# Matmul operands of an encoder layer placed at different remainders modulo 256 bytes

## The chip, the cores and the metric

The kernel runs on one core of a Trainium2 chip. The metric is the device time of one execution in microseconds (us), from the first to the last instruction with what lies around them. A core has five engines that run side by side: TensorE (PE, with weight loads shown as PEld), VectorE (DVE), ScalarE (ACT), GpSimd (POOL) and SyncE (SP), and 16 DMA engines. All of them meet in the on-chip memory SBUF: 128 partitions, and along each partition a row of bytes. This case is about where along that row a buffer starts.

## The reference

One layer of a bidirectional encoder, on 512 tokens of width 2048, in float32:

```python
xn = rmsnorm(h, norm1_g)
z_f, q, k, v, gate_f, gate_a = split(xn @ w_in)          # widths 1024, 2048 (five times)
y_f = Re(2-D DFT of z_f over tokens and channels of a group) @ w_fourier
y_a = rmsnorm(differential attention of q, k, v) * (1 - lambda_init) @ w_attn
h = h + (sigmoid(gate_f) * y_f + sigmoid(gate_a) * y_a) @ w_out
hn = rmsnorm(h, norm2_g)
# PEER: 8 heads, product keys, the best 16 of 16384 experts for each head and token
act = gelu(hn . expert_u[idx]) * softmax(top_scores)
h = h + sum(act * expert_v[idx])
```

## The kernel before

**Three matmuls for one.** Each float32 operand is split into a high part (rounded to the type fp32r, by a cast on ACT) and a low part (the rest, by a subtraction on DVE). `mm3` (lines 138 to 141) then issues three matmuls: high by high (L139), high by low (L140), low by high (L141). In a matmul the first operand is stationary: a weight load puts its 128 columns into the array. The second operand moves: its columns stream through the array. Rows of the trace write `out<-moving,stationary`, so `vb<-atl,whi` streams `atl` over weights `whi`. The weights of the next matmul are loaded while the present one streams.

**The stream of weights.** All weights come as 1 MB pieces (128 x 2048 float32) through one ring, made by `fetch`, `high`, `low` and `take`: `raw` (by DMA), `whi` (L112, ACT) and `wlo` (L117, DVE), three buffers each, in the pool `gran`. `take` hands out piece i, and has the high part of piece i+2 made, the low part of i+1, and piece i+4 fetched.

**The stages, in order.** Fourier branch, attention heads, gates, projections and queries: matmuls that write `mm`, with 512, 256 or 258 moving columns; the activations lie in `ah0..3` and `al0..3` (pool `act`), stationary in some stages and moving in others. Then the scores: 128 blocks of experts, of 48 matmuls each, `mm<-ah,whi` with 352 moving columns: the experts are evaluated densely for 352 of the 512 tokens. The other 160 gather their experts' rows by indirect DMA and work on them on DVE, beside these matmuls. The result of each block goes through gelu to the scratch `s_d`. Last the values: for each pair n of blocks `weigh` multiplies the scores `st` by the routing weights `gt` and casts the product to `ath` (L1027); `weigh_low` makes `atl` (L1033). Five buffers each, of two blocks (index `ee`) side by side:

```python
        h = pool.tile([P, 2, SD], F32R, name="ath", bufs=5)     # SD = 352 columns
        nc.scalar.copy(h, st)
```

They move through weights from `expert_v`, into eight PSUM banks `vb`; `add_up` (L1083) adds the banks to `accT`. In this stage too, DVE sums gathered rows (`acc`, L1073).

**Where the buffers start.** Pools stack tile after tile, and SBUF is full to its end. In the pool `act`, on the right end, a filler `shim` of 56 float32 lies behind the activations. Worked out from the tiles' sizes, these starts modulo 256 bytes follow (the first column of a slice within a `whi`, `wlo`, `ah` or `al` lies a multiple of 512 bytes behind the start of its tile):

| tile | before | after the change |
|---|---|---|
| whi (3 buffers) | 0, 0, 0 | 0, 64, 128 |
| wlo (3 buffers) | 0, 0, 0 | 64, 128, 128 |
| ah, al (4 each) | 0 | 128 |
| ath, ee = 0 (5 buffers) | 0 each | 0, 0, 0, 64, 224 |
| ath, ee = 1 | 128 each | 64, 64, 64, 128, 32 |
| atl, ee = 0 | 0 each | 0, 64, 128, 0, 160 |
| atl, ee = 1 | 128 each | 64, 128, 192, 64, 224 |
| raw (3 buffers), accT, acc, row | 0, 224, 224, 224 | the same |

Before, the half `ee` = 1 starts 352 columns or 1408 bytes, that is 5.5 times 256, behind the half `ee` = 0.

The order of the instructions is written out by hand, engine by engine (`manual_schedule`), so that waits alone move them in time.

Of the kernel before, what the change touches and what calls it, by code (L numbers as in the profile page):

```python
# [9 lines left out]
F32 = mybir.dt.float32  # L10
F32R = mybir.dt.float32r
# [5 lines left out]
P = 128  # L17
S = 512
D = 2048
# [12 lines left out]
SD = S - G0  # L32
# [3 lines left out]
COL = {2: 0, 3: P, 1: 2 * P, 0: 3 * P}  # L36
FH = 258
R = 8


@with_exitstack
def tile_encoder_layer(ctx: ExitStack, tc: tile.TileContext, x, g1, g2, qkg, sg, lv, nd, cs, cc,
                       w8, wz, wqkv, wgf, wga, wf, wa, wo, wq, keys, up, eu, ev, g2r, out):
    nc = tc.nc
# [6 lines left out]
    gran = pool_of(ctx, "gran", 3)  # L51
    act = pool_of(act_ctx, "act", side="right")
# [15 lines left out]
    def f32(ap):  # L68
        return ap.bitcast(F32)
# [20 lines left out]
                    "(e p) d -> p e d", p=P))  # L90
    raws, his, los, at, V = {}, {}, {}, [0], {}

    def fetch(i):
        if i < len(stream):
            raw = gran.tile([P, D], F32, name="raw")
            src = stream[i]
            nc.sync.dma_start(raw if len(src.shape) == 2 else raw.rearrange("p (a b) -> p a b", a=2), src)
            raws[i] = raw
# [8 lines left out]
    def high(i):  # L107
        if i in folds:
            fold(i)
        if i < len(stream):  # L110
            his[i] = gran.tile([P, D], F32R, name="whi")
            nc.scalar.copy(his[i], raws[i])  # L112

    def low(i):
        if i < len(stream):
            los[i] = gran.tile([P, D], F32R, name="wlo")
            nc.vector.tensor_sub(los[i], raws.pop(i), f32(his[i]))  # L117

    def take(k):
# [99 lines left out]
    dots2 = const.tile([P, G2], F32, name="dots2")  # L219
    qks = few[:, 11:11 + HEADS + 1]  # L220
    xnT = new_act()
    shim = act.tile([P, 56], F32, name="shim")
    nc.vector.memset(shim, 0.0)

    def first_group(pool, spare, junk, done):

        rows, guesses, rstd, banks = [], {}, {}, [bank("mm") for _ in range(4)]
        for tb in range(NT):
            rows.append(pool.tile([P, D], F32, name=f"x{tb}"))
            for i in range(2):  # L230
                sl = slice(i * 1024, i * 1024 + 1024)
                nc.sync.dma_start(rows[tb][:, sl], x[tb * P:(tb + 1) * P, sl])
            if tb == 0:
                fetch(0)
        nc.gpsimd.dma_start(g1s, g1)
        nc.gpsimd.dma_start(g2s, g2)
        nc.gpsimd.dma_start(sgs, sg)
        nc.gpsimd.dma_start(qkgs, qkg)
        fetch(1)
        fetch(2)  # L240

        def measure(tb):
            sums = pool.tile([P, 4], F32, name=f"xs{tb}")
            for i in range(4):
                square_sum(rows[tb][:, i * 512:(i + 1) * 512], sums[:, i:i + 1], junk)
            guesses[tb] = row_guess(pool, sums, f"n1{tb}")

        def rows_of(n):
            k4, tb = divmod(n, NT)
            return k4, tb, rows[tb][:, k4 * 512:k4 * 512 + 512]  # L250

        def scale(n):
            k4, tb, src = rows_of(n)
            if k4 == 0:
                rstd[tb] = rms_refine(guesses[tb])
            nc.vector.tensor_scalar(src, src, rstd[tb], None, op0=ALU.mult)

        def turn(n):
            src = rows_of(n)[2]
            turned[n] = bank("tr")  # L260
            for k in range(4):
                nc.tensor.transpose(turned[n][:, k * P:(k + 1) * P], src[:, k * P:(k + 1) * P], ident)

        def place(n):
            k4, tb, _ = rows_of(n)
            xg = spare[:, n % 2].rearrange("p (k t) -> p k t", k=4)
            nc.vector.tensor_tensor(xg, turned.pop(n).rearrange("p (k t) -> p k t", k=4),
                                    g1s[:, 4 * k4:4 * k4 + 4, None].to_broadcast([P, 4, P]), op=ALU.mult)
            h, l = xnT[k4]
            bs = slice(tb * P, (tb + 1) * P)  # L270
            split(xg, h[:, :, bs], l[:, :, bs])

        def quarter(i, q, parts="hl"):
            sl = slice(q * 512, q * 512 + 512)
            if i not in his:
                his[i], los[i] = gran.tile([P, D], F32R, name="whi"), gran.tile([P, D], F32R, name="wlo")
            if "h" in parts:
                nc.scalar.copy(his[i][:, sl], raws[i][:, sl])
            if "l" in parts:
                nc.vector.tensor_sub(los[i][:, sl], raws[i][:, sl], f32(his[i][:, sl]))  # L280
            if "l" in parts and q == 3:
                raws.pop(i)
                fetch(i + 3)

        turned = {}
        measure(0)
        for q in range(4):
            quarter(0, q, "h")
        scale(0)
        turn(0)  # L290
        quarter(0, 0, "l")
        place(0)
        for q in range(1, 4):
            quarter(0, q, "l")
        measure(1)
        plan = {(0, 3): "s1 t1 m2 p1", (1, 0): "s2 t2 m3 p2", (2, 0): "s3 t3 p3 s4 s5", (2, 2): "t4 p4",
                (3, 0): "t5 p5 s6 s7"}
        plan[12, 2] = "t15 p15"
        for n in range(4, 13):
            plan[n, 0] = f"t{n + 2} p{n + 2}" + (f" s{n + 4}" if n < 12 else "")  # L300
        for n in range(16):
            gi, tb = divmod(n, NT)
            if tb == 0 and gi < 3:
                wh, wl = (t.pop(gi).rearrange("p (k c) -> p k c", k=4) for t in (his, los))
                at[0] += 1
            elif tb == 0:
                wh, wl = take(4)
            bs = slice(tb * P, (tb + 1) * P)
            for kk in range(4):
                ah, al = kslice(xnT, gi * 4 + kk)  # L310
                mm3(banks[tb], (ah[:, bs], al[:, bs]), (wh[:, kk, :], wl[:, kk, :]),
                    gi == 0 and kk == 0, gi == 3 and kk == 3)
                for word in plan.get((n, kk), "").split():
                    i = int(word[1:])
                    {"s": scale, "t": turn, "p": place, "m": measure}[word[0]](i)
            if n in (2, 3):
                quarter(1, 2 * n - 4)
                quarter(1, 2 * n - 3)
            if 4 <= n < 12:
                quarter(n // 4 + 1, n % 4)  # L320
            if n == 11:
                high(4)
            if gi == 3:
                done(tb, banks[tb])
# [6 lines left out]
    with ExitStack() as so:  # L331
        with ExitStack() as st:
            pool = pool_of(st, "p1z")
# [687 lines left out]
    def weigh(n):  # L1021
        ck, e2 = pairs[n]
        st = sts[n]
        sv = st.rearrange("p e (c t) -> p e c t", t=GT)
        nc.vector.tensor_mul(sv, sv, gts[ck][:, :, 2 * e2:2 * e2 + 2, :].rearrange("p c e t -> p e c t"))
        h = pool.tile([P, 2, SD], F32R, name="ath", bufs=5)
        nc.scalar.copy(h, st)  # L1027
        ats[n] = h

    def weigh_low(n):  # L1030
        h, st = ats[n], sts.pop(n)
        l = pool.tile([P, 2, SD], F32R, name="atl", bufs=5)
        nc.vector.tensor_sub(l, st, f32(h))  # L1033
        ats[n] = (h, l)

    load_weights(0)
# [55 lines left out]
    for i in range(NE):  # L1092
        ck, j = divmod(i, R)
        half, e2 = divmod(j, R // 2)
        vh, vl = take(2)
        for job in owed:
            add_up(*job)
        owed = []
        if e2 == 0:
            banks = []  # L1100
        h, l = ats[ck * 4 + e2]
        for dt in range(8):
            ds_ = slice(dt * P, dt * P + P)
            if e2 == 0:
                banks.append(vps.tile([P, 512], F32, name="vb")[:, :SD])
            for ee in range(2):
                mm3(banks[dt], (vh[:, ee, ds_], vl[:, ee, ds_]), (h[:, ee, :], l[:, ee, :]),
                    e2 == 0 and ee == 0, e2 == R // 2 - 1 and ee == 1)
        n = ck * 4 + made[j] if j in made else len(pairs)
        if n < len(pairs):  # L1110
            weigh(n)
        if j == 2 and ck > 0:
            load_weights(ck + 1)
        given += shares[j]
        gather.to(given / total)
        if n < len(pairs):
            weigh_low(n)
            load_scores(n + 3)
        if e2 == R // 2 - 1:
            for dt in range(4):  # L1120
                add_up(ck, half, dt, banks[dt])
            owed = [(ck, half, dt, banks[dt]) for dt in range(4, 8)]
        if i == NE - 4:
            gather.to(1.0)
            for t0, n, col in ((2 * P - G2, G2, None), (2 * P, P, COL[2]), (3 * P, P, COL[3]), (P, P - G2, COL[1])):
                row = accp.tile([P, D], F32, name="row", bufs=4)
                nc.sync.dma_start(row[:n], rows_d[t0:t0 + n])
                finals.append((t0, n, col, row))
# [113 lines left out]
```

## Time and profile before

| | us |
|---|---|
| median of 3 runs (3842.77, 3864.57, 3866.42) | 3864.57 |
| the profiled execution: its own time | 3845.72 |
| its span, from the first to the last instruction | 3843.9 |
| PE busy in the span | 3792.6 |
| DVE busy | 2621.2 |
| ACT busy | 1457.9 |

The three runs lie in two places, some 22 us apart; the profiled execution agrees with the lower. A matmul's row shows a duration of some 320 ns, but matmuls are pipelined: the next one starts 155 to 165 ns behind. The pace of PE is therefore read from the starts, or from how many matmuls fall into a window, and not from the durations. A count in a window takes in about two more than the window's length holds, those that reach over its edges.

### The profile page before, as it was taken

How to read it: one execution, taken by the hardware profiler on the slowest of the kernel's cores; microseconds unless marked ns; L12 is line 12 of the kernel's file. 1: busy time of each engine (PE TensorE's matmuls, PEld its weight loads, DVE VectorE, ACT ScalarE, POOL GpSimd, SP SyncE). 2: the span in 40 equal slices, each digit the busy share in tenths (PEclk: the TensorE clock that was granted, in tenths of full speed). 3: DMA queues.
4: the chain of work that ended last, by engine and by line, in shares of the span. 5: the costliest groups of instructions: out<-in, count | busy, mean ns of one | idle time of the engine just before them, and what ended most of it. 6: DMA issues, size and time to landing. Idle time of an engine off the chain costs nothing.

```text
span 3843.9 us, 53562 instructions
## 1 busy us (share of the span) xinstructions
PE 3792.6 (99%) x22055; PEld 3528.4 (92%) x22055; DVE 2621.2 (68%) x3759; ACT 1457.9 (38%) x1966; POOL 684.5 (18%) x415
## 2 busy tenths in 40 slices
PE   8999999999999999999999999999999999999999
PEld 6888888888888888889999999999999999999998
DVE  5544465555523342578996887897758999999995
ACT  4322333333322122323237638837933223223231
POOL 0000011111100000000241232232213323332330
PEclk9999999999999999999999999999999999999999
DMA  4333222222234342425998898998989999999994
GB/s 165 111 142 135 71 83 99 73 82 83 83 105 152 121 153 99 164 91 172 360 372 299 317 365 315 346 364 314 329 311 389 360 368 371 356 378 368 376 358 166
DMA packets 214188, 900.11 MB, mean 234 GB/s; under 512 B 16556, under 2 KB 94476, under 8 KB 132108
## 3 DMA queue, kind: packets, MB, share of 16 engines
q1 hardware_dynamic: 145856, 519.34, 36.8%
q0 software_dynamic: 46960, 339.81, 22.7%
q10 hardware_dynamic: 21128, 37.53, 2.7%
q8 instruction: 174, 2.85, 0.3%
q14 instruction: 70, 0.57, 0.0%
HBM read 831.31 MB, written 65.27 MB: 233 GB/s over the span
## 4 chain that ended last, share of the span: by engine, by line
PE 91%; issue 3%; DMA 2%; ACT 2%; DVE 1%; POOL 0%; ACTq 0%; DVEq 0%; SPq 0%; POOLq 0%
PE mm L139 20%; PE mm L141 20%; PE mm L140 20%; PE vb L139 8%; PE vb L140 8%; PE vb L141 8%; PE tr L872 2%; DMA g_d<-gs 1%; PE tr L139 1%; PE tr L140 1%; PE tr L141 1%; ACT whi L112 0%; DMA row<-in_ev_dram,idx 0%; PE tr L564 0%; ACT rb L888 0%
## 5 line engine op out<-in xcount | busy, mean ns | idle before, releaser
L112 ACT CAST whi<-raw 128x2048 fp32r<-128x2048 f32 x395 | 754.3, 1910 | 1277.6 <-PE vb L140 387.0
L117 DVE TENSOR_TENSOR wlo<-raw,whi 128x2048 fp32r<-128x2048 f32 x395 | 901.8, 2285 | 320.4 <-ACT whi L112 319.7
L139 PE MATMUL mm<-ah,whi 128*128 128x352 f32 (+1 forms) x3072 | 1080.1, 352 | 0.0
L141 PE MATMUL mm<-ah,wlo 128*128 128x352 f32 (+1 forms) x3072 | 1061.9, 346 | 6.5 <-DVE wlo L117 6.5
L140 PE MATMUL mm<-al,whi 128*128 128x352 f32 (+1 forms) x3072 | 1061.9, 346 | 0.0
L139 PE MATMUL vb<-ath,whi 128*128 128x352 f32 x2048 | 660.6, 323 | 1.6 <-ACT accT L1081 1.6
L141 PE MATMUL vb<-ath,wlo 128*128 128x352 f32 x2048 | 655.6, 320 | 1.2 <-DVE wlo L117 1.2
L140 PE MATMUL vb<-atl,whi 128*128 128x352 f32 x2048 | 655.9, 320 | 0.0
L141 PEld LDWEIGHTS mm<-ah,wlo 128*128 128x128 f32 x3072 | 579.4, 189 | 47.2 <-DVE wlo L117 6.8
L140 PEld LDWEIGHTS mm<-al,whi 128*128 128x128 f32 x3072 | 580.9, 189 | 39.1
L139 PEld LDWEIGHTS mm<-ah,whi 128*128 128x128 f32 x3072 | 580.2, 189 | 39.0 <-issue 0.2
L139 PE MATMUL mm<-whi,ah 128*128 128x512 f32 (+1 forms) x1408 | 502.1, 357 | 3.1 <-ACT ah L129 3.1
L141 PE MATMUL mm<-whi,al 128*128 128x512 f32 (+1 forms) x1408 | 495.9, 352 | 0.0
L140 PE MATMUL mm<-wlo,ah 128*128 128x512 f32 (+1 forms) x1408 | 495.1, 352 | 0.0
L139 PEld LDWEIGHTS vb<-ath,whi 128*128 128x128 f32 x2048 | 384.0, 188 | 1.9 <-ACT accT L1081 1.9
L141 PEld LDWEIGHTS vb<-ath,wlo 128*128 128x128 f32 x2048 | 383.7, 187 | 1.7 <-DVE wlo L117 1.7
L140 PEld LDWEIGHTS vb<-atl,whi 128*128 128x128 f32 x2048 | 384.7, 188 | 0.0
L1066 POOL DMA_INDIRECT row<-in_ev_dram,idx x128 | 246.1, 1923 | 468.6 <-DVE acc L1073 445.4
L1073 DVE SCALAR_TENSOR_TENSOR acc<-row,w,acc 128x2048 f32<-128x2048 f32 x128 | 300.5, 2347 | 12.3 <-DMA row<-in_ev_dram,idx 11.1
L141 PEld LDWEIGHTS mm<-whi,al 128*128 128x128 f32 x1408 | 267.0, 190 | 37.4 <-DVE al L130 0.7
L139 PEld LDWEIGHTS mm<-whi,ah 128*128 128x128 f32 x1408 | 267.2, 190 | 36.3 <-ACT ah L129 3.8
L140 PEld LDWEIGHTS mm<-wlo,ah 128*128 128x128 f32 x1408 | 267.7, 190 | 33.0
(323 smaller groups left out, 3708.3 us busy)
## 6 DMA issues: line engine op xcount, KB each, us to landing
raw<-in_up_dram SPq DMA_DIRECT2D x128, 1024.0 KB
raw<-in_ev_dram SPq DMA_DIRECT2D x128, 1024.0 KB
raw<-in_wqkv_dram SPq DMA_DIRECT2D x48, 1024.0 KB
s_d<-ge ACTq DMA_DIRECT2D x128, 176.0 KB
g_d<-gs SPq DMA_DIRECT2D x22, 1024.0 KB
gt<-g_d SPq DMA_DIRECT2D x16, 1408.0 KB
st<-s_d SPq DMA_DIRECT2D x64, 352.0 KB
raw<-in_wgf_dram SPq DMA_DIRECT2D x16, 1024.0 KB
```

Of the source, the lines that this page charges most:

```text
L112: nc.scalar.copy(his[i], raws[i])
L117: nc.vector.tensor_sub(los[i], raws.pop(i), f32(his[i]))
L139: nc.tensor.matmul(ps, ah, bh, start=first, stop=False, skip_group_check=shared)
L140: nc.tensor.matmul(ps, ah, bl, start=False, stop=False, skip_group_check=shared)
L141: nc.tensor.matmul(ps, al, bh, start=False, stop=last, skip_group_check=shared)
L872: nc.tensor.matmul(ps[:, t % 4], rb, ra, start=True, stop=True)
L1066: nc.gpsimd.indirect_dma_start(out=rows[s], out_offset=None, in_=ev, in_offset=bass.IndirectOffsetOnAxis(ap=jobs[s][0], axis=0))
L1073: nc.vector.scalar_tensor_tensor(acc, rows.pop(s), w, acc, op0=ALU.mult, op1=ALU.add)
```

## The change

Every buffer of `whi`, `wlo`, `ath` and `atl` becomes a tile with a name of its own and one buffer, used in the same turn as before (i modulo 3, n modulo 5). Between some of them lie fillers (`gap`, each written once by a memset on DVE), by `HGAP`, `LGAP` and two fillers of 64 bytes in `gran`. `shim` gives up the 128 bytes that these two take, and all between the two ends, `ah` and `al` too, moves by 128. The two halves of `ath` and `atl` are 400 instead of 352 columns apart, and each is made by an instruction of its own.

```diff
+HGAP = [4, 2, 0, 0, 1]
+LGAP = [2, 4, 6, 0, 0]
...
+    def gap(pool, name, n):
+        if n:
+            nc.vector.memset(pool.tile([P, 8 * n], F32, name=name, bufs=1), 0.0)
+
+    def part(name, i):
+
+        if (name, i) in (("wlo", 0), ("wlo", 1)):
+            gap(gran, f"gap{i}", 2)
+        return gran.tile([P, D], F32R, name=f"{name}{i % 3}", bufs=1)
...
-            his[i] = gran.tile([P, D], F32R, name="whi")
+            his[i] = part("whi", i)
...
-            los[i] = gran.tile([P, D], F32R, name="wlo")
+            los[i] = part("wlo", i)
...
-    shim = act.tile([P, 56], F32, name="shim")
+    shim = act.tile([P, 24], F32, name="shim")
...
-        h = pool.tile([P, 2, SD], F32R, name="ath", bufs=5)
-        nc.scalar.copy(h, st)
+        k = n % 5
+        if n < 5:
+            gap(pool, f"hgap{k}", HGAP[k])
+        h = pool.tile([P, 2 * SD + 48], F32R, name=f"ath{k}", bufs=1)
+        h = [h[:, :SD], h[:, SD + 48:]]
+        for ee in range(2):
+            nc.scalar.copy(h[ee], st[:, ee])
         ats[n] = h
...
-        l = pool.tile([P, 2, SD], F32R, name="atl", bufs=5)
-        nc.vector.tensor_sub(l, st, f32(h))
+        k = n % 5
+        if n < 5:
+            gap(pool, f"lgap{k}", LGAP[k])
+        l = pool.tile([P, 2 * SD + 48], F32R, name=f"atl{k}", bufs=1)
+        l = [l[:, :SD], l[:, SD + 48:]]
+        for ee in range(2):
+            nc.vector.tensor_sub(l[ee], st[:, ee], f32(h[ee]))
...
-                mm3(banks[dt], (vh[:, ee, ds_], vl[:, ee, ds_]), (h[:, ee, :], l[:, ee, :]),
+                mm3(banks[dt], (vh[:, ee, ds_], vl[:, ee, ds_]), (h[ee], l[ee]),
```

On DVE, towards the end of the stage of the values, this stands in a row before (`acc` is the sum of gathered rows, `iw` holds their weights):

```order
L1083 TENSOR_TENSOR accT<-vb,accT 128x352 x4
L1025 TENSOR_TENSOR st<-st,gt 128x704
L1073 SCALAR_TENSOR_TENSOR acc_23815<-row,iw_91,acc_23815 128x2048
L1033 TENSOR_TENSOR atl<-st,ath 128x704
L117 TENSOR_TENSOR wlo<-raw,whi 128x2048
```

and at the same place now:

```order
L1106 TENSOR_TENSOR accT<-vb,accT 128x352 x4
L1038 TENSOR_TENSOR st<-st,gt 128x704
L1096 SCALAR_TENSOR_TENSOR acc_23831<-row,iw_91,acc_23831 128x2048
L1056 TENSOR_TENSOR atl_31384<-st,ath_31378 128x352 x2
L130 TENSOR_TENSOR wlo_31391<-raw,whi_31311 128x2048
```

Nothing has moved; the subtraction of 704 columns has become two of 352, in the same place ahead of the next `wlo`. On ACT, in the same stage, before:

```order
L1027 CAST ath<-st 128x704
L112 CAST whi<-raw 128x2048 x4
L1027 CAST ath<-st 128x704
L112 CAST whi<-raw 128x2048
L1027 CAST ath<-st 128x704
```

and now:

```order
L1045 CAST ath_30909<-st 128x352 x2
L125 CAST whi_30923<-raw 128x2048
L125 CAST whi_30985<-raw 128x2048
L125 CAST whi_31046<-raw 128x2048
L125 CAST whi_31115<-raw 128x2048
L1045 CAST ath_31170<-st 128x352 x2
L125 CAST whi_31181<-raw 128x2048
```

Here too only the cast to `ath` is in two. The matmuls stand on PE in the same order as before, and POOL and SP issue the same.

## Rows read from the trace of the kernel before

**Rows 1.** The page: busy us and instructions; DMA in 40 slices.

```profile
PE 3792.6 (99%) x22055; PEld 3528.4 (92%) x22055; DVE 2621.2 (68%) x3759; ACT 1457.9 (38%) x1966; POOL 684.5 (18%) x415
...
DMA  4333222222234342425998898998989999999994
```

**Rows 2.** Groups of instructions on PE, shapes apart: xcount, busy us, mean ns, idle before.

```profile
L139 PE MATMUL mm<-ah,whi 128*128 128x352 f32 x2048 | 678.6, 331 | 0.0
...
L139 PE MATMUL vb<-ath,whi 128*128 128x352 f32 x2048 | 660.6, 323 | 1.6 <-ACT accT L1081 1.6
...
L141 PE MATMUL vb<-ath,wlo 128*128 128x352 f32 x2048 | 655.6, 320 | 1.2 <-DVE wlo L117 1.2
L139 PE MATMUL mm<-ah,whi 128*128 128x512 f32 x1024 | 401.5, 392 | 0.0
...
L139 PE MATMUL mm<-whi,ah 128*128 128x512 f32 x896 | 356.7, 398 | 3.1 <-ACT ah L129 3.1
...
L139 PE MATMUL mm<-whi,ah 128*128 128x256 f32 x512 | 145.4, 284 | 0.0
```

**Rows 3.** Windows: busy us and count by engine, clock, DMA share.

```profile
412.00:428.00 16.00, 16.00 (x136) 16.00 (x135) 7.72 (x11) 2.74 (x3) 2.98 (x1) 1.00 0.38 132
1140.00:1500.00 360.00, 360.00 (x1590) 298.06 (x1590) 119.20 (x82) 88.75 (x67) 0.00 (x0) 1.00 0.36 132
1755.00:1815.00 60.00, 60.00 (x374) 60.00 (x373) 53.65 (x133) 20.89 (x20) 3.48 (x3) 1.00 0.53 178
2185.00:2270.00 85.00, 85.00 (x534) 85.00 (x533) 82.55 (x105) 29.58 (x26) 29.84 (x16) 1.00 0.97 371
3000.00:3400.00 400.00, 400.00 (x2519) 400.00 (x2518) 364.51 (x280) 117.14 (x78) 133.31 (x68) 1.00 0.94 370
```

**Rows 4.** Timeline of PE where the granted clock was 0.5: start, us.

```profile
1829.03 0.49 PE L141 MATMUL mm<-ah,wlo 128*128 128x352 f32 x1
1829.32 0.49 PE L139 MATMUL mm<-ah,whi 128*128 128x352 f32 x1
1829.62 0.49 PE L140 MATMUL mm<-al,whi 128*128 128x352 f32 x1
```

**Rows 5.** Timeline of PE in the stage of the values: half ee = 1, then ee = 0.

```profile
3400.32 0.32 PE L139 MATMUL vb<-ath,whi 128*128 128x352 f32 x1
3400.48 0.32 PE L140 MATMUL vb<-atl,whi 128*128 128x352 f32 x1
3400.63 0.32 PE L141 MATMUL vb<-ath,wlo 128*128 128x352 f32 x1
3400.79 0.32 PE L139 MATMUL vb<-ath,whi 128*128 128x352 f32 x1
3400.95 0.32 PE L140 MATMUL vb<-atl,whi 128*128 128x352 f32 x1
3401.12 0.32 PE L141 MATMUL vb<-ath,wlo 128*128 128x352 f32 x1
3401.27 0.32 PE L139 MATMUL vb<-ath,whi 128*128 128x352 f32 x1
```

**Rows 6.** Timeline of PE in an attention head: twelve matmuls, first and last start.

```profile
458.58 0.28 PE L140 MATMUL tr<-vl,aTh 128*128 128x256 f32 x1
...
459.89 0.39 PE L139 MATMUL mm<-whi,ah 128*128 128x512 f32 x1
```

**Rows 7.** Timeline of PE in the Fourier stage: ten matmuls, first and last.

```profile
186.94 0.28 PE L140 MATMUL mm<-yl,whi 128*128 128x258 f32 x1
...
188.03 0.28 PE L140 MATMUL mm<-yl,whi 128*128 128x258 f32 x1
```

**Rows 8.** Groups on DVE in the stage of the values.

```profile
L1083 DVE TENSOR_TENSOR accT<-vb,accT 128x352 f32<-128x352 f32 x239 | 115.3, 519 | 61.1 <-PE vb L141 59.0 <-issue 1.5
...
L1033 DVE TENSOR_TENSOR atl<-st,ath 128x704 fp32r<-128x704 f32 x62 | 55.1, 889 | 38.3 <-ACT ath L1027 38.2
```

**Rows 9.** Groups on ACT in the same stage.

```profile
L1027 ACT CAST ath<-st 128x704 fp32r<-128x704 f32 x62 | 48.1, 776 | 7.6 <-DVE st L1025 7.6
L1081 ACT COPY accT<-vb 128x352 f32<-128x352 f32 x16 | 6.2, 460 | 0.9 <-PE vb L141 0.9
```

**Rows 10.** The window of that stage.

```profile
2848.00:3827.00 979.00, 976.21 (x6141) 975.34 (x6140) 856.84 (x648) 289.41 (x205) 307.04 (x161) 1.00 0.91 354
```

More of the change, by code (lines that the diff above doesn't have):

```diff
@@ L275, in quarter @@
             if i not in his:
-                his[i], los[i] = gran.tile([P, D], F32R, name="whi"), gran.tile([P, D], F32R, name="wlo")
+                his[i], los[i] = part("whi", i), part("wlo", i)
             if "h" in parts:
```

## The prediction

> **What bounds the kernel now.** Read the page first: PE is busy for 99% of the span [rows 1]. Then the groups on PE: nearly no idle time stands before them [rows 2]. So PE's own pace is the time, and this change, which leaves the matmuls and their order as they are, can only act through the spacing of one matmul from the next. That spacing is read from windows in which PE never idles: length by count, less the two at the edges. Five of them [rows 3]: 16.0/134 = 119.4 ns with 256 moving columns, 360/1588 = 226.7 with 512, 60/372 = 161.3 and 85/532 = 159.8 with 352 (early and later in the scores), and 400/2517 = 158.9 with 352 in the values. The granted clock there is 1.00, the level of 2.4 GHz, at which a column each cycle would be 106.7, 213.3 and 146.7 ns. What is above that I call the excess: 12.7, 13.4, 14.6, 13.1 and 12.2 ns. At the other level there is none: with the clock at 0.5 the starts are 0.29 to 0.30 us apart [rows 4], and 352 columns at 1.2 GHz are 293.3 ns. So some 13 ns of each matmul are lost at the full clock alone, and not to columns. Of all spacings there are 6144 of the scores, 6144 of the values, 3072 + 2688 with 512 columns and 1536 with 256 (three lines for each group of rows 2): 19,584 matmuls, some 250 us of excess.
>
> **Does the excess depend on placement?** Before the change nearly all operands start at remainder 0. The one large exception is the half ee = 1 in the values, at 128. There the spacings aren't alike: 0.16, 0.15, 0.16, 0.16, 0.17, 0.15, with 0.95 us for six [rows 5], where the scores, same shape and all at 0, take 0.96 or 0.97 by their windows [rows 3]. Three matmuls of six have a moving start that differs from that of their weights, and the mean is 160.0 - 158.9 = 1.1 ns lower. Two smaller places point both ways. In the heads the moving `vh`, `vl` start at 192 and the stationary parts at 64 (from their tiles' sizes): (459.89 - 458.58)/11 = 119.1 ns, an excess of 12.4 [rows 6]. In the Fourier stage the moving parts start at steps of 8 bytes from 64 to 152 against weights at 0: (188.03 - 186.94)/9 = 121.1 ns for 258 columns, an excess of 13.6 [rows 7]. And the two windows of the scores differ by 1.5 ns with the very same addresses [rows 3]: a rhythm between loads and streams can, it seems, lock in two ways. So placement matters, by one or two ns, and no row shows a place where it matters by much more for long.
>
> The Trainium skill says otherwise: its page "TensorE: Matmul & The Clock Gate", Part 2, Step-by-step, gives PE two independent read ports in SBUF, so that loading the next weights takes nothing from the running matmul. By that rule starts would not matter at all, and the sum below would be 0. The trace doesn't agree: the spacings of rows 5 vary with the half.
>
> **The change part by part.**
>
> *The matmuls.* I price a matmul whose moving and stationary starts differ, against one whose starts agree, by the values before: 1.1 ns on average with half of them unequal, so 2.2 ns each. Counting the pairs after the change from the starts: in the scores moving 128 meets weights at 0, 64, 128, and 3440 of 6144 pairs (56%) are unequal; with 512 columns 1568 of 3072 and 1312 of 2688; with 256 columns 1280 of 1536; in the values 4696 of 6144 (76%), before it was 3072. Gains: scores 3440 x 2.2 = 7.6 us; 512 columns 2880 x 2.2 = 6.3; 256 columns 1280 x 2.2 = 2.8; values (4696 - 3072) x 2.2 = 3.6. The early scores ran in the slower rhythm [rows 3], I take it a quarter of them; with six weight buffers at three starts I expect that lock to break: 1536 x 1.3 = 2.0 us. Sum 22.3 us. Bounds: were every spacing of 352 columns the shortest that recurs [rows 5] (0.15 us as rounded; I take 155 ns), it would be 5 ns x 13,440 for all that are at remainder 0 now and 3.9 x 6144 in the values, 91 us less; were all in the slow rhythm, 161.3, it would be 1.3 x 13,440 + 2.4 x 6144 = 32 us more. I stay near the values' average and not near either end, as it alone is a mean over thousands of matmuls with mixed starts.
>
> *Two instructions for one.* A subtraction of 704 columns takes 889 ns on DVE, one of 352 at most the 519 of the addition to accT, which has an operand in PSUM [rows 8]: 2 x 519 - 889 = 149 ns more, 62 times in this stage, 9.2 us. On ACT 2 x 460 - 776 = 144 ns [rows 9], 62 times, 8.9 us. From below both are 0, since columns stay the same and a second start costs something. I take the upper ends. DVE has 979 - 857 = 122 us idle in the stage, ACT 690 [rows 10]; behind `atl` on DVE queue the next `wlo`, for which PE waited only 1.2 us [rows 2], made more than a block (48 x 159 = 7.6 us) ahead. So nothing of it lies on PE's path; were that cover gone, DVE's 9.2 us would be the price.
>
> *Fillers.* Eight memsets of at most 48 columns, each below the 519 ns of 352 columns [rows 8]: under 4 us on DVE, once, hidden likewise. The names with one buffer each are reused after the same number of turns as before, so no wait is added; POOL and SP have the same queues. DMA is busy for 0.94 to 0.97 of the two late windows [rows 3], so a PE faster by more than about 4% would meet it; 22 us are 0.6%.
>
> **Sum.** The profiled execution took 3845.7 us; less 22 it is 3824. The median of the three runs is 3864.6, 19 above the profiled one; on that footing 3842, which I give as the forecast.
>
> **The rivals.**
>
> *Conflicts nearly gone.* If agreement of starts between the load and the stream is the whole cause of the excess and the new starts keep them apart, the spacing goes to 155 or below everywhere: 91 us, 3774 on the median's footing; half of that, 3819, already counts here. For it: one recurring step of the values is there, and the excess is absent at the lower clock, so there is something to remove. Against it: 44% of the pairs in the scores still agree, and in rows 7 no start agrees and the excess is 13.6.
>
> *Placement is free* (or: one excess goes where another came). Rows 6 and 7 speak for it, with 12.4 and 13.6 on either side of the 13.3 at equal starts. Then the time is the median, 3865, give or take what separates the runs. The Trainium skill's rule above ("TensorE: Matmul & The Clock Gate", Part 2) would give this.
>
> *A slower rhythm everywhere.* The early scores kept the rhythm of 161.3 through a window of 60 us with starts as in the later one [rows 3]. If mixed starts put most of the scores and values into such a rhythm, or into the 13.6 of rows 7 and above, PE loses 32 us (3897 on the median's footing). It decides from a mean excess above 13.3 ns in the scores. Against it: the values, where starts mix, are the fastest of the 352-column windows.
>
> **How the numbers follow.** A measurement of this kernel can tell about 1%, 39 us, from no change. The forecast (-10 to -38 us) gets 0.35; conflicts nearly gone (beyond -38) 0.33; placement free (-10 to +10) 0.2; slower rhythm 0.12, most of it below 39 us as well, the rest by a rhythm still slower than any window's. Faster by over 1%: 0.33; within 1%: 0.58; slower: 0.09. For eight in ten the range takes in most of the first rival, to 3780, and the free placement with the spread of the runs, to 3873.
>
> **What would show it.** In the profile after: windows without idle time, in the scores a mean below 159 and in the values below 158.5; spacings that differ from block to block as the buffers turn (15 combinations of 3 and 5 in the values), where they repeated before; PE's excess at the 1.2 GHz level still 0. Two casts of about 0.4 us each in place of one of 0.78, and PE's waits for `wlo` still about a microsecond. I am wrong if the scores stay at 160 in all their windows (placement free), if a window's mean rises over 161, or if waits of PE for `wlo` or DMA grow to tens of us.

## The result, and the profile after

The changed kernel took 3871.75 us (median of 9 runs, 3869.54 to 3878.67), the kernel before 3846.01 (9 runs, 3840.35 to 3866.42): a ratio of 1.0052, 95% interval 1.0037 to 1.0068. It is slower by 0.5%, where the forecast said faster by 0.6%. The profiled execution took 3869.54 us, its span is 3867.8, 23.9 above that of the profiled execution before.

The page of the profile after, answering [rows 1]:

```profile
PE 3819.5 (99%) x22055; PEld 3541.4 (92%) x22055; DVE 2627.5 (68%) x3831; ACT 1463.0 (38%) x2030; POOL 679.3 (18%) x415
...
DMA  4333222222234342424998898998989999999984
```

PE has the same 22,055 instructions and is again busy for 99%; DVE and ACT have 72 and 64 instructions more, for 6.3 and 5.1 us. The groups on PE, shapes apart, answer [rows 2]:

```profile
L152 PE MATMUL mm<-ah,whi 128*128 128x352 f32 x2048 | 676.7, 330 | 0.0
L154 PE MATMUL mm<-ah,wlo 128*128 128x352 f32 x2048 | 664.9, 325 | 6.6 <-DVE wlo L130 6.6
...
L152 PE MATMUL vb<-ath,whi 128*128 128x352 f32 x2048 | 662.6, 324 | 0.9 <-ACT accT L1104 0.9
L154 PE MATMUL vb<-ath,wlo 128*128 128x352 f32 x2048 | 661.0, 323 | 1.2 <-DVE wlo L130 1.2
...
L152 PE MATMUL mm<-ah,whi 128*128 128x512 f32 x1024 | 405.5, 396 | 0.0
...
L152 PE MATMUL mm<-whi,ah 128*128 128x512 f32 x896 | 358.2, 400 | 3.1 <-ACT ah L142 3.1
```

The last column has no new wait: 1.2 us for `wlo` in the values and 3.1 for `ah` stood before, and the 6.6 falls on one matmul of the scores, as 6.5 did before:

```profile
L141 PE MATMUL mm<-ah,wlo 128*128 128x352 f32 x2048 | 662.8, 324 | 6.5 <-DVE wlo L117 6.5
```

What changed is the pace. Windows in which PE never idles (length; busy us and count of PE, PEld, DVE, ACT and POOL; granted clock, DMA share, GB/s), answering [rows 3, 10]; the second is all 512 moving activations, the third 512 moving weights:

```profile
415.00:431.00 16.00, 16.00 (x136) 16.00 (x136) 7.59 (x13) 3.17 (x3) 2.98 (x1) 1.00 0.38 132
1083.00:1383.00 300.00, 300.00 (x1307) 245.27 (x1306) 94.25 (x62) 71.23 (x46) 0.00 (x0) 1.00 0.34 121
1388.00:1548.00 160.00, 160.00 (x695) 130.14 (x695) 46.87 (x29) 36.98 (x39) 0.00 (x0) 1.00 0.36 131
2198.00:2283.00 85.00, 85.00 (x531) 85.00 (x530) 82.18 (x103) 29.14 (x26) 27.99 (x16) 1.00 0.96 371
3014.00:3414.00 400.00, 400.00 (x2491) 400.00 (x2490) 363.25 (x301) 119.07 (x104) 133.13 (x68) 1.00 0.93 365
2862.00:3841.00 979.00, 976.86 (x6079) 976.00 (x6078) 858.78 (x705) 294.60 (x267) 305.31 (x160) 1.00 0.91 354
```

With two taken off each count: 16/134 = 119.4 ns with 256 columns, as before; 300/1305 = 229.9 and 160/693 = 230.9 with 512, where it was 226.7; 85/529 = 160.7 in the scores (159.8); 400/2489 = 160.7 in the values (158.9). In 979 us of the values stand 6079 matmuls instead of 6141 at the same clock: 62 x 160 ns = 10 us.

Within the 512 columns the spacing now turns with the three weight buffers. The timeline, at the first matmul of each block of 48 (the two blocks between the first row and the third use buffers 1 and 2, the block from the third row on buffer 0):

```profile
1218.86 0.39 PE L152 MATMUL mm<-ah,whi 128*128 128x512 f32 x1
...
1229.85 0.39 PE L152 MATMUL mm<-ah,whi 128*128 128x512 f32 x1
...
1240.75 0.40 PE L152 MATMUL mm<-ah,whi 128*128 128x512 f32 x1
...
1251.95 0.39 PE L152 MATMUL mm<-ah,whi 128*128 128x512 f32 x1
```

The activations start at 128. Weights at 64 and 128 (`whi1`, `wlo1`): (1229.85 - 1218.86)/48 = 229.0 ns. Both at 128: 10.90/48 = 227.1. At 0 and 64: 11.20/48 = 233.3. Where all starts agree, the spacing is that of before; where they don't, it is up to 6 ns longer.

**Where the 23.9 us went.** Sums over all spacings of a stage (from each matmul's start to the next start on PE, waits included) from the trace, in us, for the profiled executions of the result and for two more of each kernel, which are among the experiments below:

| stage (matmuls) | before | again | again | after | again | again |
|---|---|---|---|---|---|---|
| 512, moving weights (2688) | 626.6 | 627.7 | 627.1 | 632.4 | 632.4 | 633.5 |
| 512, moving activations (3072) | 700.9 | 700.9 | 701.1 | 709.3 | 709.6 | 708.6 |
| 256 (1536) | 184.8 | 184.9 | 184.8 | 183.8 | 183.8 | 183.8 |
| scores (6144) | 1025.2 | 1029.5 | 1023.5 | 1025.4 | 1022.6 | 1023.3 |
| values (6144) | 980.0 | 987.8 | 987.9 | 989.9 | 990.8 | 991.0 |
| span | 3843.9 | 3858.0 | 3850.7 | 3867.8 | 3864.3 | 3867.5 |

In the first pair: 5.8 + 8.4 - 1.0 + 0.2 + 9.9 = 23.3 of 23.9 us. On the mean of three: 5.6 + 8.2 - 1.0 - 2.3 + 5.3 = 15.8 of 15.7. The result's interval is 14 to 26 us.

### The profile page after: what moved, and what is told of

Its sections match the earlier page's. It is cut to its first block, busy times and chain, and to the rows that moved or that the text cites. A ratio compares the mean times of both kernels' runs of the same rounds, so it can differ in the third digit from the quotient of the medians.

```text
span 3867.8 us, 53699 instructions
## 1 busy us (share of the span) xinstructions
PE 3819.5 (99%) x22055; PEld 3541.4 (92%) x22055; DVE 2627.5 (68%) x3831; ACT 1463.0 (38%) x2030; POOL 679.3 (18%) x415
## 4 chain that ended last, share of the span: by engine, by line
PE 91%; issue 3%; DMA 2%; ACT 2%; DVE 1%; POOL 0%; ACTq 0%; DVEq 0%; SPq 0%; POOLq 0%
PE mm L152 20%; PE mm L153 20%; PE mm L154 20%; PE vb L152 8%; PE vb L154 8%; PE vb L153 8%; PE tr L885 2%; DMA g_d<-gs 1%; PE tr L152 1%; PE tr L154 1%; PE tr L153 1%; ACT whi L125 0%; DMA row<-in_ev_dram,idx 0%; PE tr L577 0%; ACT rb L901 0%
```

## The experiments

The theory after the result: a matmul of 512 columns pays for a moving start that differs from that of its weights, modulo 256; in the values, 158.9 ns was one of several spacings that the old starts allow. Rivals: the split casts and subtractions slow PE (by their traffic, not by waits); an absolute position is dear, and not a difference; the spacing of after, too, is an accident of one execution.

### Measuring the price by itself

`m1_map` issues blocks of 48 matmuls from one stretch of SBUF, with nothing else running (shortened; the markers are short matmuls between the blocks):

```python
for n in (352, 512):
    for mo in range(0, 256, 32):              # moving start
        for so in (0, 64, 128, 192):          # start of the weights
            for part in range(2):
                ...                           # 3 + part markers of 256 columns
                for i in range(48):
                    at = so // 4 + 128 * (i % 8)
                    nc.tensor.matmul(ps, w[:, at:at + 128], m[:, mo // 4:mo // 4 + n], ...)
```

> This kernel leaves out the whole layer. It runs 64 pairs of starts, each twice with 48 matmuls in a row: moving columns (352, then 512) that start at 0, 32, ..., 224 modulo 256 bytes through weights that start at 0, 64, 128, 192; nothing else runs beside them. Theory 1 (placement: what a matmul loses beside its columns is set by the start of the moving columns against the start of the weights that are loaded meanwhile): the spacing differs from pair to pair, by the traces of the two kernels from about 155 to 165 ns with 352 columns and 226 to 237 with 512; 160.0 and 226.7 where both starts agree; and it depends on the difference of the two starts alone. Rival (placement is free, and the changed kernel is slower for another reason, its split instructions or what other engines do): the same spacing, 160 and 226.7, for all pairs.

Its timeline, blocks of 512 columns; first moving 0, weights 0, then moving 0, weights 64:

```profile
531.19 11.07 PE L47 MATMUL bank<-m,w 128*128 128x512 f32 x48
542.09 0.64 PE L41 MATMUL bank<-m,w 128*128 128x256 f32 x4
...
553.82 11.37 PE L47 MATMUL bank<-m,w 128*128 128x512 f32 x48
565.03 0.62 PE L41 MATMUL bank<-m,w 128*128 128x256 f32 x4
```

(542.09 - 531.19)/48 = 227.1 ns, against 11.21/48 = 233.5. Excess over 213.3 ns, mean of the last spacings of each block and of both passes (the passes differ by about 1 at most):

| moving \ weights | 0 | 64 | 128 | 192 |
|---|---|---|---|---|
| 0 | 13.3 | 19.9 | 19.7 | 15.6 |
| 64 | 20.0 | 13.3 | 20.1 | 19.0 |
| 128 | 19.6 | 15.6 | 13.3 | 20.0 |
| 192 | 20.1 | 19.1 | 15.5 | 13.3 |

Equal starts are the cheapest of these, and with the moving start off by an odd multiple of 32 it is 19.9 to 21.1. The difference of the two starts tells nearly all, with one exception: a moving start 64 ahead costs 15.5 or 15.6 with weights at 64, 128 and 192, but 20.0 with weights at 0. And since all weights of a block start alike, the map can't tell whether a matmul's own weights count or those loaded meanwhile.

In sum this is the layer's cost, though not stage by stage. For moving activations at 128 the table gives (2 x 19.6 + 15.6)/3 = 18.3, (2 x 15.6 + 13.3)/3 = 14.8 and 13.3 for the three buffers, where the layer shows 20.0, 15.7 and 13.8; on the mean of the 64 pieces (20, 19 and 25 in the three buffers) it is 15.3, which makes (15.3 - 13.3) x 3072 = 6.1 us of the 8.2 to 8.4. For moving weights it gives (2 x 19.7 + 20.1)/3 = 19.8, (2 x 20.1 + 13.3)/3 = 17.8 and 13.3, on the mean of 56 pieces (16, 17 and 23) 16.5, or 8.6 us, of which 5.6 to 5.8 came; 14.7 us for both together, against 13.8 to 14.2. The last 768 of these matmuls pay 4.3 ns each (226.7 before, 231.0 after), but the 1344 in the heads from the second on only 1.0: they took 232.2 ns on average with equal starts already. Why is open.

With 352 columns most pairs lie at 13.3, whatever their difference. Two differences do not: a moving start 96 ahead gives 15.4 to 15.7, and 128 falls into one of two paces. So do equal starts: at 0, 64 and 192 the first pass gave 14.4 or 14.5 (161.1 ns), the second 13.3. Moving 0, weights 128, first and second pass, in the timeline:

```profile
43.16 7.76 PE L47 MATMUL bank<-m,w 128*128 128x352 f32 x48
50.76 0.65 PE L41 MATMUL bank<-m,w 128*128 128x256 f32 x4
51.25 8.15 PE L47 MATMUL bank<-m,w 128*128 128x352 f32 x48
59.23 0.52 PE L41 MATMUL bank<-m,w 128*128 128x256 f32 x3
```

7.60/48 = 158.3 ns and 7.98/48 = 166.3, with the same addresses; one marker more ahead and another PSUM bank are all that differs.

`m5_map2` is the same with weights at 0, for the order of the values (high, low, high of one half, then of the other, with every set of four starts out of 0, 64, 128, 192), for finer steps with 512 columns, and for 256 columns.

> Leaves out the whole layer. Streams alone, weights at 0: (a) 352 columns in the order of the values (high, low, high of one half, then of the other), the four starts at 0, 64, 128 or 192, all 256 combinations, twice 36 matmuls each; (b) 512 columns at fine differences of 4 to 28 bytes to either side; (c) 256 columns at eight differences. Theory 1 (difference of starts) with what the first map showed (13.3 ns of excess at equal starts and 352 columns in nearly all pairs, about 20 with 512 columns unless the starts are equal): (a) most combinations near 13.3, the one of the kernel before (0, 0, 128, 128) at 12.2 or 13.3, some as low as 9 to 11; (b) 13.3 at equal starts, up to 20 a few bytes away; (c) 10 to 13 at some differences, 13.3 at equal starts. Rival (only the rhythm into which it locked matters): the two passes of one combination differ as much as combinations do.

Over all 256 sets the mean excess was 14.2, from 10.0 to 20.0; with all four starts equal to the weights' 14.4 (behind the rise of the clock) and 13.3 in the two passes. The set of the kernel before, 0 for one half and 128 for the other, gave 13.3 in one pass and 12.2 in the other: 160.0 and 158.9 ns, in one execution. In 48 of the 256 sets the passes differ by more than 1 ns. No set lay under 12.2 on the mean of its passes; the two that came down to 10.0 once took 15.0 the other time. So there was no placement of the values worth building. With 512 columns a difference of 4 bytes cost 23.3, of 244 bytes 26.7, and of 28 or 252 bytes 13.3 again: not a matter of steps of 64. With 256 columns nothing was above the 13.3 of equal starts, and other differences went down to 6.7: there, unequal is no dearer and mostly cheaper, as the layer shows (-1.0 us).

### One part of the change at a time

`m2_split` is the kernel before with each cast and subtraction in two halves, nothing placed anew:

```diff
-        nc.scalar.copy(h, st)
+        for ee in range(2):
+            nc.scalar.copy(h[:, ee], st[:, ee])
...
-        nc.vector.tensor_sub(l, st, f32(h))
+        for ee in range(2):
+            nc.vector.tensor_sub(l[:, ee], st[:, ee], f32(h[:, ee]))
```

> The kernel before with nothing but the casts to ath and the subtractions to atl made in two halves each; all starts stay. Theory 1 (placement): 0 within 3 us. Rival (the 62 extra casts and subtractions, 9 us each on ACT and DVE, lie on PE's path): +5 to +10 us, and the values' matmuls wait for wlo by as much.

3845.70 us (12 runs), ratio 0.9987 (0.9972 to 1.0001): the split costs nothing that can be measured, and that rival falls.

`m3_act128` is the kernel before with `shim` cut from 56 to 24 float32, so that every activation starts at 128 and every weight part at 0:

> The kernel before with shim alone cut to 24: the activations start at 128 modulo 256, all weights stay at 0, ath and atl stay. Theory 1, by the spacings of the changed kernel at a difference of 128: with 512 columns and moving activations +7 ns each (3072: +22 us), with 512 and moving weights +2 ns (2688: +6), with 256 and in the scores 0 to -1 (-5): in all +15 to +25 us, more than the whole change cost in these stages. Rival (split instructions): 0. Rival (weight buffers at three starts break the rhythm, so that it is their mixture that costs, not the difference): 0 to +5 us here.

3878.49 us, ratio 1.0065 (1.0041 to 1.0089): one filler's size makes 25 us (16 to 34 by the interval). The sums are 638.0 and 718.1 us with 512 columns (moving weights, moving activations), 1029.9 in the scores, and 994.4 in the values, whose starts are those of before. Its windows of 512 columns (both kinds), of the scores twice, and of the values:

```profile
1100.00:1390.00 290.00, 290.00 (x1250) 235.12 (x1249) 89.68 (x58) 69.31 (x45) 0.00 (x0) 1.00 0.33 117
1405.00:1555.00 150.00, 150.00 (x647) 121.65 (x646) 40.11 (x26) 35.03 (x38) 0.00 (x0) 1.00 0.30 111
1885.00:2010.00 125.00, 125.00 (x791) 125.00 (x790) 122.59 (x200) 41.00 (x36) 43.90 (x24) 1.00 0.94 359
2200.00:2320.00 120.00, 120.00 (x722) 120.00 (x721) 106.83 (x138) 38.52 (x34) 32.20 (x21) 1.00 0.92 351
3014.00:3414.00 400.00, 400.00 (x2485) 400.00 (x2484) 360.84 (x276) 115.65 (x77) 137.24 (x69) 1.00 0.93 362
```

With 512 columns 290/1248 = 232.4 and 150/645 = 232.6, an excess of 19.1 and 19.2 as in the table for a difference of 128 (19.6, 19.7). The scores go at 125/789 = 158.4 in one stretch and at 120/720 = 166.7 in another, one program and one set of addresses: the two paces of `m1_map`. Up to 1849 us it had been 166.7 as well; the change of pace came behind a wait of PE and a dip of the granted clock to 0.5.

`m4_values` is the change with weights and activations at 0, so that only `ath` and `atl` are placed anew (no `gap` in `part`, `shim` 56, the first of `HGAP` 0 instead of 4); `m7_weights` is the change with `weigh`, `weigh_low` and their `mm3` as before, so that only weights and activations are (`ath` and `atl` lie 128 further on behind the two fillers of `gran`, at 128 and 0 instead of 0 and 128):

> The change to the values alone: ath and atl placed as in the changed kernel, modulo 256, and split; weights at 0 and activations at 0 as before. Theory 1: all stages ahead as before, the values slower by up to 1.7 ns a matmul as in the changed kernel: 0 to +10 us, without waits of PE. If the mixture of weight starts is what costs in the values, 0 or below. Rival (split instructions): the same as the kernel with the split alone.

> The changed kernel with the values' buffers made as before (one cast, no fillers): weights at 0, 64, 128 and activations at 128 remain. Theory 1: the stages with 512 columns lose 5 to 6 us with moving weights and 8 to 9 with moving activations, 256 columns gain 1, scores within 5; the values, with moving starts of 128 and 0 through weights at 0, 64, 128, lose 0 to 10: in all +12 to +25 us. Rival (split instructions or the fillers of the values): about 0.

3853.74 us, ratio 1.0008 (0.9991 to 1.0024), and 3864.90 us, ratio 1.0037 (1.0023 to 1.0050). The two parts add up, 0.08% + 0.37% = 0.45%, to the 0.52% of the whole within the intervals. In `m7_weights` the 512-column stages took 633.3 and 709.2 us, as after, and the values 988.5; in `m4_values` they took 626.3 and 701.0, as before, and the values 990.8. The weights and activations carry most of the loss.

`m6_halves` is the kernel before with the halves of `ath` and `atl` 384 columns apart, so that all operands start at 0:

```diff
-        h = pool.tile([P, 2, SD], F32R, name="ath", bufs=5)
+        h = pool.tile([P, 2, SD + 32], F32R, name="ath", bufs=5)[:, :, :SD]
```

> The kernel before with the halves of ath and atl 384 instead of 352 columns apart: all four starts at 0, as the weights. Theory 1: the values at 160.0 ns, where the kernel before showed 158.9 in one execution and the one with split casts, of the same starts, 160.0 in another: 0 to +7 us. If the alternation of halves is worth nothing (both were rhythms of one arrangement): 0.

3853.66 us, ratio 1.0011 (0.9998 to 1.0024); values 987.2 us, 160.0 ns each. Making all pairs equal gained nothing, and cost at most 0.24%.

`m8_shift` is the kernel before with a filler of 128 bytes at the head of `gran` and `shim` 24, so that every operand moves by 128 alike:

> The kernel before with everything moved by 128 bytes alike: whi, wlo, ah, al, ath, atl all start 128 further, differences stay. Theory 1 (the difference alone matters): 0 within 6 us, the spread of the runs. Rival (the absolute start matters, so that activations at 128 cost by themselves): +15 to +30 us, as the kernel with activations alone at 128.

3841.84 us, ratio 0.9983 (0.9967 to 0.9998), with 627.1, 700.9, 184.8, 1021.1 and 981.4 us in the five stages: what it was at 0. So differences between starts matter in the layer, and a shift of all by 128 bytes does not.

### The same program again

`m9_before_again1`, `m10_before_again2`: the kernel before, unchanged; `m11_after_again1`, `m12_after_again2`: the changed kernel.

> The kernel before, unchanged, profiled once more. If the spacing of a matmul were fixed by the starts of its operands alone (the prediction's step), the 6,144 matmuls of the values would take 980.0 us in sum again (mean excess 12.2 ns) and the span would be within 1 us of 3843.9. If the same starts allow more than one rhythm, and each execution settles into one, the values come out near 987 to 990 us (excess 13.3 to 13.5) in some executions, the scores at 1021 to 1030, and the span moves by as much; the 512-column stages, at equal starts, stay at 626.6 and 700.9 us in both theories.

> The kernel before a third time. As for the run ahead of it: 980.0 us in the values again if the starts alone fix the spacing, either of 980 and 987 to 990 us if an execution can settle into one of two rhythms.

> The changed kernel, profiled once more. The price of unequal starts in the 512-column matmuls should come back in every execution: 632.4 us and 709.3 us within 1.5 us each, with the 256-column stage at 183.8. If that too were a matter of the rhythm an execution settles into, one or both would fall back towards 626.6 and 700.9 us. The values may lie anywhere from 985 to 992 us.

> The changed kernel a third time, for the same: 632.4 and 709.3 us again if unequal starts cost the 512-column matmuls in every execution.

They took 3859.77, 3852.48, 3866.12 and 3869.29 us; their sums stand in the table of the result. A window of the values in `m9_before_again1`, the same stretch as the last of [rows 3]:

```profile
3000.00:3400.00 400.00, 400.00 (x2502) 400.00 (x2501) 362.29 (x277) 117.12 (x78) 136.83 (x70) 1.00 0.94 367
```

400/2500 = 160.0 ns, where the row of before, the same program, has 158.9. `m10_before_again2` shows 2502 as well. The windows of `m12_after_again2` that answer to the second, third and fifth of after:

```profile
1083.00:1383.00 300.00, 300.00 (x1307) 245.26 (x1306) 93.32 (x61) 71.22 (x46) 0.00 (x0) 1.00 0.33 121
1388.00:1548.00 160.00, 160.00 (x695) 130.11 (x695) 46.90 (x29) 37.85 (x40) 0.00 (x0) 1.00 0.34 129
3014.00:3414.00 400.00, 400.00 (x2491) 400.00 (x2490) 363.19 (x301) 119.30 (x104) 133.29 (x68) 1.00 0.94 365
```

The counts are those of after to the last matmul, in this execution and in `m11_after_again1`. So the price of unequal starts comes back each time, while the pace of the old values, and of the scores (1023.5 to 1029.5), does not. It can change within one execution, too. In the profiled execution of before, PE waits three times early in the values. First and last starts of the two stretches between these waits, 46 and 68 matmuls long:

```profile
2864.67 0.32 PE L139 MATMUL vb<-ath,whi 128*128 128x352 f32 x1
...
2871.87 0.32 PE L139 MATMUL vb<-ath,whi 128*128 128x352 f32 x1
...
2873.12 0.32 PE L139 MATMUL vb<-ath,whi 128*128 128x352 f32 x1
...
2883.77 0.32 PE L140 MATMUL vb<-atl,whi 128*128 128x352 f32 x1
```

(2871.87 - 2864.67)/45 = 160.0 ns, then (2883.77 - 2873.12)/67 = 159.0; the 5926 matmuls behind the third wait keep 158.9. In `m9_before_again1` and `m10_before_again2` three and two of the three early stretches run at 158.9, and the long one at 160.0. The experiments ran on three chips; two paces in one execution show that the chip alone doesn't decide. So the pace can be settled anew behind a wait, and the last stretch is 96% of the stage.

## Why the prediction was wrong

**The bound and the place: right.** PE's spacing is the time, no wait was added, and 23.3 of the 23.9 us stand in the spacings of the five stages that the prediction named.

**The price of an unequal pair: wrong, and with it the sign.** The step that failed is "1.1 ns on average with half of them unequal, so 2.2 ns each", cheaper than an equal pair. It failed twice. First, the 158.9 of [rows 3, 5] was not the price of those starts but one pace among several: the same execution has a stretch at 160.0 earlier in the values, the same program gave 160.0 in two further executions, the same six starts gave both paces in `m5_map2`, and `m3_act128` ran at 161.1 with the same starts (400/2483 in the last row of its windows). Against 160.0 in the scores there was then nothing to explain. The prediction had seen two rhythms with the very same addresses in the scores, and yet took a difference of 1.1 ns in the values for an effect of their addresses. Second, that price of 352 columns was carried to 512, for which before had no unequal pair in any row. There it is +2.3 to +6.7 ns instead of -2.2.

Term by term, the first size the prediction's, the second measured on the mean of three executions: 512 columns -6.3, +13.8 us; scores -9.6 (7.6 for the pairs, 2.0 for the early rhythm), -2.3, which is less than they differ between executions of one kernel; 256 columns -2.8, -1.0 (the right sign, a third of the size); values -3.6, +5.3. For the values, 989.9 to 991.0 us recurs with the new starts in four executions (`m4_values` among them), and the old ones gave 980.0 to 987.9 in five (with `m2_split` and `m8_shift`), but 994.4 in a sixth, `m3_act128`. So the 9.9 us of the first pair are in part the luck of a fast pace before, and a loss by the new starts of the values is not shown; `m4_values`, at 1.0008 (0.9991 to 1.0024), shows none either. Which of the mixed starts make the excess of 14.0 ns there is not settled; the mean of the sets in `m5_map2`, 14.2, lies next to it.

**Two read ports.** By the Trainium skill's page "TensorE: Matmul & The Clock Gate" (Part 2, Step-by-step), with its two independent read ports, placement would be free. The prediction was right to doubt that, though by a row that didn't show it: `m1_map`, with no other engine at work, has 13.3 and 19.9 ns for two starts of the same weights. How the two reads disturb each other no run here shows.

**The covers: right.** Split casts, subtractions and fillers cost PE nothing (`m2_split`, and no new wait). Their rows, answering [rows 8, 9], in the stage of the values:

```profile
L1056 DVE TENSOR_TENSOR atl<-st,ath 128x352 fp32r<-128x352 f32 x124 | 59.3, 520 | 32.0 <-ACT ath L1045 31.2
L98 DVE MEMSET lgap<- 128x48 f32 x1 | 0.1, 98 | 0.0
L1045 ACT CAST ath<-st 128x352 fp32r<-128x352 f32 x124 | 53.8, 481 | 7.6 <-DVE st L1038 7.6
```

One takes 520 and 481 ns, as sized; busy time grew by 59.3 - 55.1 = 4.2 and 53.8 - 48.1 = 5.7 us, under the 9.2 and 8.9 allowed, since two in a row overlap. A filler takes 98 ns.

**The rivals.** "A slower rhythm everywhere" came nearest, with the right sign, but its place was wrong: it decides in the scores, and their excess stayed (13.7 before, 13.9 after), while the loss came with 512 columns, to which its price gave the same 1.3 ns as to all others, and which took 13.8/5760 = 2.4 ns more on average. Nothing of "conflicts nearly gone" came. "Placement is free" holds for the scores, and for the values nothing else is shown.

**The footing.** The forecast stood on the median of three runs, 3864.6. Over nine runs beside the changed kernel the median is 3846.0, so that footing was 19 us too high, and only thereby did the range hold the result. The two places of the runs are largely the paces: `m9_before_again1` is 14.1 us longer than the profiled one, of which the values make 7.8 and the scores 4.3.

**What would show it.** Spacings that differ from block to block did come, and were named as a sign that the forecast was right; they are there with the opposite sum. Of the signs of being wrong, the scores at 160 did come: 160.7 in the window. At a granted clock of 0.5 the starts are again 0.30 us apart, as in [rows 4]:

```profile
1842.99 0.50 PE L152 MATMUL mm<-ah,whi 128*128 128x352 f32 x1
1843.29 0.50 PE L153 MATMUL mm<-al,whi 128*128 128x352 f32 x1
```

## What to carry to other kernels

Where PE streams without a pause, the starts of moving and stationary operands modulo 256 belong to the tuning: with 512 columns, equal starts are a cheap and sure choice (226.7 ns in an unbroken stream against 232 to 233 at a difference of 128), and one filler of 128 bytes in the wrong place made 25 us of 3850. Measure such a price by itself, in the width it is wanted for, before carrying it over: the sign was another with 256 and with 512 columns. And before a difference of 1 ns in a pace is put down to the program, profile the same program again, and compare its stretches between waits.

## What the runs showed of the hardware

- At the 2.4 GHz level a stream of matmuls at equal starts mostly keeps a spacing 13.3 ns above its columns, for 256, 352 and 512 columns alike; in the heads, with 512, equal starts gave 232.2 ns on average, waits included.
- With 512 columns most unequal starts gave 15.5 to 26.7 ns above the columns instead; differences of 28 and 252 bytes (weights at 0) were as cheap as 0. With 256 columns unequal starts gave 6.7 to 13.3.
- With 352 columns the same addresses can run at two paces, 158.3 or 166.7 ns at a difference of 128, 160.0 or 161.1 at equal starts, 158.9 or 160.0 (161.1 once) in the values with both mixed. Where a pace was seen to change, something had interrupted the stream: other matmuls, or a wait (at 2864 us in the values of 0.65 us, without a dip of the clock).
